# Turning four of eight token tiles to channel layout with VectorE block transposes and SBUF transfers in the w_out stage

## The chip, the cores and the metric

The kernel runs on one core of one Trainium2 chip. The core has five engines that run side by side and meet through semaphores: TensorE (matmuls and transposes, with a separate weight load), VectorE, ScalarE, GpSimd and SyncE. Here SyncE (queue SP) issues nearly all DMAs. Each engine takes its instructions in the order in which they were put on its queue. The metric is the device time of one execution in microseconds (us), as the median over runs.

## The reference, cut to what matters

One layer of a hybrid decoder over 1024 tokens with 16 meta tokens ahead of them, 1024 channels, float32. Two mixers (convolution and windowed attention) are merged by gates; then

```python
mixed = jax.nn.sigmoid(g_attn) * y_attn + jax.nn.sigmoid(g_conv) * y_conv
h = layer_norm(DEEPNORM_ALPHA * h + mixed @ w_out, ln1_g, ln1_b)
up = causal_dwconv(h @ ffn_w_up, ffn_dw, ffn_dw_b)
u, g = jnp.split(up, 2, axis=-1)
f = (jax.nn.gelu(g, approximate=False) * u) @ ffn_w_down
return layer_norm(DEEPNORM_ALPHA * h + f, ln2_g, ln2_b)
```

The norm runs over the channels of a token, so it wants tokens on the partitions. The product with `ffn_w_up` sums over channels, so it wants channels on the partitions. Between the two, `h` is turned.

## The kernel before, in words

A float32 product is done as three products of parts rounded to a shorter form (high by high, high by low, low by high; `product`, lines 304 to 316). Splitting a tensor into its parts is a cast on ScalarE and a subtraction on VectorE.

The stage around the change is the product with `w_out`. The 1024 tokens make eight tiles of 128, taken in the order 3, 7, 2, then two edge rows (called -1), then 6, 0, 4, 1, 5 (line 1480). For one tile, `out_rows` (line 1319) does this:

- it loads the residual rows from `h0d` into one of two row buffers `RT`, which is `OB` columns 0 to 2047, the two taken in turn, so that the load for a tile needs the buffer of the tile two before it;
- TensorE makes two halves of 512 columns, 24 matmuls each, into a PSUM bank `ps_w` (three banks in turn);
- VectorE adds each half to the residual (L1342) and takes its statistics (L1343); the norm follows: aggregate (L246), reciprocal root on ScalarE (L253), three small steps (L261 to L263) and the scaling (L1364);
- SyncE stores the rows to `h1d`.

`turn` (line 1373) then turns the tile: eight 128x128 transposes on TensorE (L1378) into two PSUM banks `ps_h`, and eight activations on ScalarE (L1388) that read them, apply the norm's gain and bias per channel and write `FA`, the channel layout `h1F`. The loop hands a finished tile to the next call of `out_rows` (`ahead`), so a tile is turned while TensorE works on the next one: after that one's first half, tile 3 after the second half. Tile 5, the last, is turned inside the next stage.

The next stage multiplies by `ffn_w_up` with a seven-product scheme on 2x2 blocks. It needs sums and differences of the blocks of `FA` (`form_t2`, `form_t3`, `form_t4`, L1288) and their parts (`bsplit`: cast L1279, subtraction L1284). The tokens stand in two halves, sub 1 (tiles 2, 3, 6, 7) and sub 0 (tiles 0, 1, 4, 5; its first columns, `EARLY`, are tiles 0 and 4). These steps run during the products of tiles 0, 4, 1 and 5 (the `work` table, line 1476), with the first weight splits (L1409, L1426). The first products of the next stage (L1599) are those of sub 1; those of sub 0 follow.

Order: every instruction carries a priority number (`rank`; `RK_TURN` is 450, lower goes first), from which a planner with its own time model puts each engine's instructions in order. `line` (line 1257) fixes the order of a list of VectorE instructions by hand: those of tiles 0, 4, 1, 5, the splits and the sums stand in it. `after` fixes the order of two instructions on one engine. `load` (line 112) issues a DMA on SyncE's queue.

Of the kernel before, what the change touches and what calls it, by code (L numbers as in the profile page):

```python
# [25 lines left out]
AF = mybir.ActivationFunctionType  # L26
# [3 lines left out]
P = 128  # L30
D = 1024
KC = D // P
# [29 lines left out]
SUB = [(0, 258), (258, HW)]  # L62


RK_TURN, RK_SPLIT, RK_EVAC, RK_START, RK_QKV, RK_RESID, RK_ATT = 450, 500, 600, 1000, 10000, 20000, 30000
# [36 lines left out]
def tile_hybrid_layer(  # L102
# [3 lines left out]
    nc = tc.nc  # L106
# [5 lines left out]
    def load(o, i):  # L112
        return nc.sync.dma_start(out=o, in_=i)
# [5 lines left out]
    def f32(ap):  # L119
        return ap.bitcast(F)  # L120

    def after(ins, first):

        tc.add_manual_dep(ins.ins, first.ins.name, mybir.DependencyInfo(
            mybir.DependencyClass.NoSync, mybir.DependencyReason.SCHED_ONLY), reason="order of work")

    @contextmanager
    def rank(p):

        saved = tc.cur_priority  # L130
        tc.cur_priority = p
        yield
        tc.cur_priority = saved
# [10 lines left out]
    RHC = arena.tile([P, 8384], R, name="RHC")  # L144
    RHO = arena.tile([P, 8384], R, name="RHO")
    OB = arena.tile([P, 4 * U], F, name="OB")
# [49 lines left out]
    cols = const.tile([P, N_COLS], F, name="cols")  # L196
# [19 lines left out]
    g1col = lambda k: colA[:, 58 + k:59 + k]  # L216
    b1col = lambda k: colA[:, 66 + k:67 + k]
# [60 lines left out]
    def split(raw, hi, lo, quick=False, behind=None):  # L278
        ins = nc.scalar.copy(hi, raw)  # L279
        if behind is not None:  # L280
            after(ins, behind)
        return (nc.vector if quick else nc.gpsimd).tensor_tensor(lo, raw, f32(hi), OP.subtract)  # L282
# [391 lines left out]
    bias = ap.tile([P, 2, NH // 2, KW], F, name="bias")  # L674
# [58 lines left out]
    for r in range(2):  # L733
        rows = slice(r * HD, (r + 1) * HD)
# [13 lines left out]
    src = ps[:16, :P].rearrange("p (g d) -> p g d", d=HD)  # L748
    nc.scalar.copy(VA[:16, 0, :, 0], src)
    nc.vector.tensor_tensor(VA[:16, 0, :, 1], src, f32(VA[:16, 0, :, 0]), OP.subtract)  # L750
    for q4 in range(2):
# [4 lines left out]
        src = ps[:, :].rearrange("p (n g d) -> p n g d", g=2, d=HD)  # L756
# [16 lines left out]
    def load_q(g, i):  # L773
        m = 0 if i else 16
        t = ap.tile([P, 8 * P + 16], R, name="qt", tag="qt", bufs=3)[:, 16 - m:]
        for h in range(2):
            load(f32(t[h * HD:(h + 1) * HD]), dram(qd, g * HD * 8 * U + q_at(i) - m, [[8 * U, HD], [1, 8 * P + m]]))
        if m:
            pairs0.append(t[:, :16].rearrange("p (l r q) -> p l r q", l=2, r=4))
        return t[:, m:].rearrange("p (u l h x) -> p l u h x", l=2, u=2, h=2)  # L780
# [7 lines left out]
    ahead = chunks_done[first_chunk + 2 * KC + 7]  # L788
# [6 lines left out]
    for h in range(NH):  # L795
        g, r = divmod(h, 4)
        o = ps[:2, h * 16:(h + 1) * 16]
# [34 lines left out]
    for g in range(NKV):  # L832
# [3 lines left out]
        src = ps[:16].rearrange("p (r q) -> p r q", r=4)[:, :, 0:2]  # L836
# [3 lines left out]
    for g in range(NKV):  # L840
        o = po[:, g * 8:g * 8 + 8]
# [21 lines left out]
    for i in range(NB):  # L863
        for g in range(NKV):
            q = load_q(g, i) if i else q0[g]
# [6 lines left out]
            for u in range(2):  # L872
# [3 lines left out]
                for h in range(2):  # L876
                    o = ps[:, h * KW:h * KW + w]
# [8 lines left out]
                if not i:  # L886
                    f = first[u]
                    src = ps[:, :2 * KW].rearrange("p (h c) -> p h c", h=2)
# [9 lines left out]
            for h in range(2):  # L898
                for u in range(2):
                    j = h * 2 + u  # L900
# [68 lines left out]
    OC = late.tile([P, 8320], R, name="OC")  # L969
# [169 lines left out]
    def two_rows(k, behind=None):  # L1139

        for t, a in enumerate(two_sum):
            m = pair[:, k, t:t + 1]
            if k == 0:
                nc.scalar.activation(a, wo_raw[k], AF.Copy, scale=m)
                continue
            ins = nc.vector.scalar_tensor_tensor(a, wo_raw[k], m, a, OP.mult, OP.add)
            if behind is not None:
                after(ins, behind)
# [74 lines left out]
    def h1_at(sub, i):  # L1223
        return 2048 * sub + i * (SUB[sub][1] - SUB[sub][0])

    def h1F(sub, h, k):
        o = h1_at(sub, h * KC + k)
        return FA[:, o:h1_at(sub, h * KC + k + 1)]
# [28 lines left out]
    def line(ins):  # L1257

        if lined:
            after(ins, lined[-1])  # L1260
        lined.append(ins)
        return ins
# [33 lines left out]
    def form_t2(sub, cs=slice(None)):  # L1296
        b11, b12, b21, b22 = blocks(sub)
        bsub(b11, b12, b11, cs)
        bsub(T2_AT[:, :b22.shape[1]], b22, b11, cs)

    def form_t3(sub, cs=slice(None)):
        b11, b12, b21, b22 = blocks(sub)
        bsub(b12, b22, b12, cs)

    def form_t4(sub, cs=slice(None)):
        b11, b12, b21, b22 = blocks(sub)
        bsub(b21, T2_AT[:, :b22.shape[1]], b21, cs)

    def split_of(sub, q, cs=slice(None)):
        b11, b12, b21, b22 = blocks(sub)  # L1310
        src = {B11: b11, B21: b21, BT2: T2_AT[:, :b22.shape[1]], BT4: b21, BT1: b11, BT3: b12, B22: b22}[q]
        bsplit(sub, q, src, cs)
# [76 lines left out]
        return behind[-1] if behind else None  # L1389


    RING = [RHO[:, i * 1024:(i + 1) * 1024] for i in range(4)]
    RING += [None] * 4
    RING += [RHO[:, 6208 + i * 1024:6208 + (i + 1) * 1024] for i in range(2)]
    ring_next, W2 = [0], []

    def wsplit(src):
# [4 lines left out]
        else:  # L1402
            i = (i - 2) % len(RING)
            if RING[i] is None:
                RING[i] = wsp_p.tile([P, D], R, name="ws", tag=("whi", "wlo")[i % 2])
            t = RING[i]
        hi, lo = t[:, 0:512], t[:, 512:1024]
# [59 lines left out]
    def edges():  # L1467
        with rank(RK_TURN):
            first, second = (FA[:, h * 2064:h * 2064 + 2064].rearrange("p (k n) -> p k n", n=258)[:, :, 0:2]
                             for h in range(2))  # L1470
            for t, c, op in ((edge, 58, OP.mult), (first, 66, OP.add)):
                line(nc.vector.tensor_tensor(first, t, colA[:, c:c + KC].unsqueeze(2).to_broadcast([P, KC, 2]), op))
            nc.vector.memset(second, 0.0)

    ahead = []
# [4 lines left out]
    for i in (3, 7, 2, -1, 6, 0, 4, 1, 5):  # L1480
        if i == -1:
            out_rows(i)
            continue
        rows = out_rows(i, ahead, work.get(i, ()))
        ahead = [None, (i, *rows)] if i == 3 else [(i, *rows)]
        if i == 3:
            two_rows(7, rows[2])
        if i == 7:
            for a, (hi, lo) in zip(two_sum, two_parts):
                after(split(a, hi, lo, True), rows[2])  # L1490
            two_stack.close()
            W2.append(wo_stack.enter_context(tc.tile_pool(name="w2", bufs=1, side="right", reuse_waits="tile")).tile(
                [P, 2048], R, name="W2"))
        if i == 0:
            form_t2(1)
        if i == 4:
            split_of(1, BT4)
            split_of(1, BT1)
            edges()
        if i == 1:  # L1500
            split_of(1, BT3)
            split_of(0, B21, EARLY)
            form_t3(0, EARLY)
            form_t4(0, EARLY)
# [64 lines left out]
    for c in range(FC):  # L1569
# [8 lines left out]
        for subs in passes:  # L1578
            last = subs == passes[-1]
            w_next = iter(range(7))  # L1580
            a, b = SUB[subs[0]][0], SUB[subs[-1]][1]
            i = max(a, 2)

            def at(t, a=a):
                return t[:, 254 + a:254 + b]
# [19 lines left out]
            def tt(*x):  # L1605
                with rank(RK_CHAIN):
                    return nc.vector.tensor_tensor(*x)
# [12 lines left out]
            ins = tt(c11[:, a:b], at(Z), u13[:, a:b], OP.add)  # L1620
# [23 lines left out]
            ins = tt(c22[:, i:b], c22[:, i:b], u13[:, i:b], OP.add)  # L1644
# [127 lines left out]
    rows, stats = {}, {}  # L1772
# [158 lines left out]
```

## Time and profile before

| | |
|---|---|
| time, median of 3 runs | 1236.12 us (1236.04 to 1236.16) |
| the profiled execution: span from its first to its last instruction | 1234.6 us |
| what a run's time has beside that span | 1.5 us (1236.12 - 1234.6) |
| TensorE busy | 1225.2 us, 99% |
| VectorE busy | 1085.2 us, 88% |
| ScalarE busy | 584.7 us, 47% |
| GpSimd busy | 15.6 us, 1% |
| mean granted TensorE clock | 0.999 |

The profile gives no time of its own for the profiled execution other than the span. In its lines PE is TensorE, PEld its weight load, DVE is VectorE, ACT ScalarE, POOL GpSimd, SPq the queue of SyncE; L1378 is line 1378 of the kernel. A row of a timeline has the start, the duration, the engine, the line, the operation, output from input, shapes and a count, and in brackets the idle time before it and what ended it. A busy share is an average over the whole span; the chain that ended last says what a change in one place can be worth.

### The profile page before, as it was taken

How to read it: one execution, taken by the hardware profiler on the slowest of the kernel's cores; microseconds unless marked ns; L12 is line 12 of the kernel's file. 1: busy time of each engine (PE TensorE's matmuls, PEld its weight loads, DVE VectorE, ACT ScalarE, POOL GpSimd, SP SyncE). 2: the span in 40 equal slices, each digit the busy share in tenths (PEclk: the TensorE clock that was granted, in tenths of full speed). 3: DMA queues.
4: the chain of work that ended last, by engine and by line, in shares of the span. 5: the costliest groups of instructions: out<-in, count | busy, mean ns of one | idle time of the engine just before them, and what ended most of it. 6: DMA issues, size and time to landing. Idle time of an engine off the chain costs nothing.

```text
span 1234.6 us, 21810 instructions
## 1 busy us (share of the span) xinstructions
PE 1225.2 (99%) x8568; PEld 1141.5 (92%) x8568; DVE 1085.2 (88%) x1842; ACT 584.7 (47%) x1065; POOL 15.6 (1%) x20
## 2 busy tenths in 40 slices
PE   9999999999999999999999999999999999999997
PEld 8999989999999999888999999999999998888886
DVE  8899989999879798659899999998999986996697
ACT  7532336654255223345755545555455554445331
POOL 1000000000000010000000000000000000000000
PEclk9999999999999999999999999999999999999999
DMA  7396834412255655322255555554455568988722
GB/s 282 74 298 151 210 98 116 127 55 73 82 158 163 183 140 144 104 85 87 66 171 207 191 187 205 188 183 142 172 203 190 178 239 304 391 315 312 256 86 85
DMA packets 109152, 213.02 MB, mean 173 GB/s; under 512 B 31883, under 2 KB 46779, under 8 KB 108922
## 3 DMA queue, kind: packets, MB, share of 16 engines
q1 hardware_dynamic: 93050, 200.56, 49.5%
q10 hardware_dynamic: 16000, 11.07, 2.9%
q8 instruction: 67, 1.10, 0.4%
q14 instruction: 35, 0.29, 0.1%
HBM read 149.98 MB, written 62.70 MB: 172 GB/s over the span
## 4 chain that ended last, share of the span: by engine, by line
PE 98%; DVE 1%; ACT 0%; issue 0%; DMA 0%; POOL 0%; DVEq 0%; POOLq 0%
PE px L1599 14%; PE py L1599 9%; PE ps_x L1745 9%; PE ps_z L315 8%; PE ps_z L314 8%; PE ps_z L310 8%; PE ps_z L1745 8%; PE pw L1599 5%; PE pz L1599 5%; PE ps_p L310 2%; PE ps_p L314 2%; PE ps_p L315 2%; PE ps_w L310 2%; PE ps_w L315 2%; PE ps_w L314 2%; PE ps_z L550 2%
## 5 line engine op out<-in xcount | busy, mean ns | idle before, releaser
L707 DVE SCALAR_TENSOR_TENSOR FA<-cin,cols,FA 128x1026 f32<-128x1026 f32 x120 | 152.2, 1277 | 0.9
L315 PE MATMUL ps_z<-RHO,wlo 128*128 128x256 f32 (+2 forms) x324 | 103.5, 320 | 0.0
L314 PE MATMUL ps_z<-RHO,whi 128*128 128x256 f32 (+2 forms) x324 | 103.4, 319 | 0.0
L315 PE MATMUL ps_z<-RHC,wlo 128*128 128x256 f32 (+2 forms) x324 | 103.4, 319 | 0.0
L314 PE MATMUL ps_z<-RHC,whi 128*128 128x256 f32 (+2 forms) x324 | 103.4, 319 | 0.0
L310 PE MATMUL ps_z<-RHO,whi 128*128 128x256 f32 (+2 forms) x324 | 103.3, 319 | 0.0
L310 PE MATMUL ps_z<-RHC,whi 128*128 128x256 f32 (+2 forms) x324 | 103.2, 319 | 0.0
L279 ACT CAST whi<-wr 128x1024 fp32r<-128x1024 f32 x37 | 38.9, 1050 | 107.4 <-PE ps_z L314 85.5
L1408 ACT CAST RHO<-wr 128x512 fp32r<-128x512 f32 x92 | 55.3, 619 | 25.3 <-DVE wr L1426 11.7
L1409 DVE TENSOR_TENSOR RHO<-wr,RHO 128x512 fp32r<-128x512 f32 x92 | 61.8, 684 | 5.1 <-ACT RHO L1408 5.0
L310 PEld LDWEIGHTS ps_z<-RHO,whi 128*128 128x128 f32 x324 | 60.9, 188 | 4.3
L314 PEld LDWEIGHTS ps_z<-RHO,whi 128*128 128x128 f32 x324 | 61.0, 188 | 4.2
L310 PEld LDWEIGHTS ps_z<-RHC,whi 128*128 128x128 f32 x324 | 60.9, 188 | 4.1
L314 PEld LDWEIGHTS ps_z<-RHC,whi 128*128 128x128 f32 x324 | 61.0, 188 | 4.0
L315 PEld LDWEIGHTS ps_z<-RHO,wlo 128*128 128x128 f32 x324 | 60.9, 188 | 4.0
L315 PEld LDWEIGHTS ps_z<-RHC,wlo 128*128 128x128 f32 x324 | 61.0, 188 | 3.9
L1426 DVE TENSOR_TENSOR wr<-wr 128x512 f32<-128x512 f32 x88 | 59.9, 681 | 0.2
L282 DVE TENSOR_TENSOR wlo<-wr,whi 128x1024 fp32r<-128x1024 f32 x35 | 42.7, 1220 | 11.8 <-ACT whi L279 11.4
L1611 ACT COPY FA<-px 128x514 f32<-128x514 f32 (+2 forms) x23 | 13.2, 572 | 70.7 <-PE px L1599 70.6
L1408 ACT CAST ws<-wr 128x512 fp32r<-128x512 f32 x60 | 36.1, 618 | 18.8 <-DVE wr L1426 10.7
L714 ACT ACTIVATE FA<-ps_z,cols 128x258 f32<-128x258 f32 (+2 forms) x48 | 26.1, 544 | 39.4 <-PE ps_z L315 36.6
L1599 PE MATMUL px<-OA,RHO 128*128 128x258 f32 (+1 forms) x336 | 43.8, 279 | 0.0
(491 smaller groups left out, 3488.2 us busy)
## 6 DMA issues: line engine op xcount, KB each, us to landing
wr<-in_w_up_dram SPq DMA_DIRECT2D x44, 512.0 KB, 4.6
wr<-in_w_z_dram SPq DMA_DIRECT2D x30, 512.0 KB, 3.9
fd<-FA SPq DMA_DIRECT2D x44, 256.0 KB, 2.4
OB<-in_w_down_dram SPq DMA_DIRECT2D x19, 512.0 KB
qt<-qd SPq DMA_DIRECT2D x28, 256.0 KB, 4.1
td<-OB SPq DMA_DIRECT2D x12, 512.0 KB
sums<-fd SPq DMA_DIRECT2D x12, 512.0 KB, 7.6
sd<-sums SPq DMA_DIRECT2D x12, 512.0 KB
```

The costliest lines, as they stand in the source:

```text
L279: ins = nc.scalar.copy(hi, raw)
L282: return (nc.vector if quick else nc.gpsimd).tensor_tensor(lo, raw, f32(hi), OP.subtract)
L310: ins = nc.tensor.matmul(ps, ah, bh, start=i == 0, stop=False)
L314: nc.tensor.matmul(ps, ah, bl, start=False, stop=False)
L315: last = nc.tensor.matmul(ps, al, bh, start=False, stop=i == n - 1)
L707: nc.vector.scalar_tensor_tensor(acc[c], cin[:, j:j + U], wc, acc[c], OP.mult, OP.add)
L714: nc.scalar.activation(t, ps, AF.Tanh, bias=bcol(14 + i), scale=0.5)
L1408: nc.scalar.copy(hi, src)
L1409: ins = nc.vector.tensor_tensor(lo, src, f32(hi), OP.subtract)
L1426: ins = nc.vector.tensor_tensor(*x)
L1599: ins = nc.tensor.matmul(o, x[:, ks], bmat(sub, q, hl, k), start=first and k + j == 0, stop=k == 3 and j == 2, skip_group_check=not first)
L1745: nc.tensor.matmul(bank[:, cs], l[:, ts], r[:, ws], start=first and a and x + k == 0, stop=z and x == len(ops) - 1 and k == 2, skip_group_ ...
```

## The change

Tiles 3, 7, 2 and 0 (`TURN_AT`) are no longer turned by `turn`. For them `turn_dma` issues, right after `out_rows`:

1. one VectorE transpose of the 128x1024 row tile in 32x32 blocks, from the row buffer into 1024 columns of `OB` (from column 2048 for tiles 3, 7 and 2, from column 3072 for tile 0), its blocks grouped by the group q of 32 channels; for tile 0 it stands in the fixed order `line`;
2. 16 DMAs on SyncE's queue, each of 32 partitions by 256 columns (1 KB a row), that move the block rows of 32 tokens to the partitions of their 32 channels, into free columns of `OC` or `RHC`;
3. eight ScalarE activations as before, which now read those columns in SBUF, in four runs of 32, in place of PSUM.

Tiles 6, 4, 1 and 5 are turned as before. Tile 3 no longer asks for the later place of its turn.

```diff
+    TURN_AT = {3: (OC, 4144, 2048), 7: (OC, 5168, 2048), 2: (OC, 6192, 2048), 0: (RHC, 2096, 3072)}
+
+    def turn_dma(i, r):
+        t, o, b = TURN_AT[i]
+        blocks, cols = OB[:, b:b + 1024], f32(t[:, o:o + 1024])
+        with rank(RK_TURN):
+            ins = nc.vector.transpose(blocks.rearrange("p (q k j) -> p q k j", q=4, k=KC),
+                                      r.rearrange("p (k q j) -> p q k j", k=KC, q=4))
+            if i in (0, 4):
+                line(ins)
+            for a in range(4):
+                for q in range(4):
+                    load(cols[32 * q:32 * q + 32, a * 256:(a + 1) * 256],
+                         blocks[32 * a:32 * a + 32, q * 256:(q + 1) * 256])
+            h, jj = divmod(i, 4)
+            sub = 0 if jj < 2 else 1
+            a = 2 + jj * P - SUB[sub][0]
+            src = cols.rearrange("p (a k j) -> p k a j", a=4, k=KC)
+            for k in range(KC):
+                nc.scalar.activation(h1F(sub, h, k)[:, a:a + P].rearrange("p (a j) -> p a j", a=4), src[:, k],
+                                     AF.Identity, bias=b1col(k), scale=g1col(k))
+
...
         rows = out_rows(i, ahead, work.get(i, ()))
-        ahead = [None, (i, *rows)] if i == 3 else [(i, *rows)]
+        ahead = [] if i in TURN_AT else [(i, *rows)]
+        if i in TURN_AT:
+            turn_dma(i, rows[0])
         if i == 3:
             two_rows(7, rows[2])
```

## The prediction

> **What bounds the kernel now.** I read the page first (engine shares, then the chain that ended last), then the pieces of that chain between 517 and 606 us, then the same stretch engine by engine.
>
> ```profile
> span 1234.6 us, 21810 instructions
> ...
> PE 1225.2 (99%) x8568; PEld 1141.5 (92%) x8568; DVE 1085.2 (88%) x1842; ACT 584.7 (47%) x1065; POOL 15.6 (1%) x20
> ...
> PE 98%; DVE 1%; ACT 0%; issue 0%; DMA 0%; POOL 0%; DVEq 0%; POOLq 0%
> ...
> 517.40 0.87 PE ps_h L1378 x8
> 522.38 0.87 PE ps_h L1378 x8
> 547.84 0.88 PE ps_h L1378 x8
> 559.62 0.87 PE ps_h L1378 x8
> ...
> 605.53 1.57 PE pw L1599 x11
> ```
>
> TensorE is 98% of the chain, and every group of eight transposes (one token tile, L1378) lies on it with 0.87 to 0.88 us. So a transpose that leaves TensorE shortens the chain, until another engine takes its place. In this stretch VectorE stands close behind:
>
> ```profile
> 512.69 2.47 DVE L1146 SCALAR_TENSOR_TENSOR two<-wr,pair,two 128x1024 f32<-128x1024 f32 x2
> ...
> 519.20 0.81 DVE L1364 TENSOR_SCALAR OB<-OB,mv,sd 128x1024 f32<-128x1024 f32 x1
> 534.10 0.81 DVE L1364 TENSOR_SCALAR OB<-OB,mv,sd 128x1024 f32<-128x1024 f32 x1
> 542.42 0.69 DVE L1342 TENSOR_TENSOR OB<-ps_w,OB 128x512 f32<-128x512 f32 x1 [4.91 <-PE ps_w L315]
> 547.88 0.69 DVE L1342 TENSOR_TENSOR OB<-ps_w,OB 128x512 f32<-128x512 f32 x1 [2.03 <-PE ps_w L315]
> 549.21 1.27 DVE L1409 TENSOR_TENSOR W<-wr,W 128x512 fp32r<-128x512 f32 x2
> 550.41 2.35 DVE L1284 TENSOR_TENSOR OC<-FA,OC 128x1024 fp32r<-128x1024 f32 x2
> 554.22 0.69 DVE L1342 TENSOR_TENSOR OB<-ps_w,OB 128x512 f32<-128x512 f32 x1 [0.32 <-PE ps_w L315]
> 586.73 0.68 DVE L1409 TENSOR_TENSOR RHO<-wr,RHO 128x512 fp32r<-128x512 f32 x1
> 589.56 0.69 DVE L1342 TENSOR_TENSOR OB<-ps_w,OB 128x512 f32<-128x512 f32 x1 [2.15 <-PE ps_w L315]
> 605.53 1.57 PE L1599 MATMUL pw<-OA,RHO 128*128 128x258 f32 x11 [0.38 <-DVE OA L1284]
> ```
>
> In the second fence (the timelines of VectorE and TensorE: start, us, what) the bracket is the idle time before an instruction. Up to 548 VectorE has gaps of 2 to 5 us in which it waits for TensorE. From 548 on it has only 0.32 at 554 and 2.15 at 589.56, beside short waits for ScalarE inside each norm. At 605.53 it is TensorE that waits, 0.38 us, for a split by VectorE. So both engines arrive at 605 together: the gain is the smaller of what TensorE and VectorE save ahead of it.
>
> **The change part by part.** *TensorE.* Four groups go (tiles 3, 7, 2, 0): 0.87 + 0.87 + 0.88 + 0.87 = 3.49 us. (Tile 2's group, near 536, is not among the rows shown; I give it the 0.88 of its neighbour.) Nothing takes their place on TensorE. Tiles 6, 4, 1, 5 keep theirs. This is the whole possible gain: no other TensorE work is touched.
>
> *ScalarE.* The same eight activations a tile, reading SBUF in four runs of 32 in place of PSUM:
>
> ```profile
> 531.10 0.29 ACT L253 ACTIVATE sd<-mv,eps 128x1 f32<-128x1 f32 x1
> 536.53 2.90 ACT L1388 ACTIVATE FA<-ps_h,cols 128x128 f32<-128x128 f32 x8 [2.17 <-PE ps_h L1378]
> 539.29 2.03 ACT L1279 CAST OC<-FA 128x1024 fp32r<-128x1024 f32 x2
> 558.81 1.05 ACT L1279 CAST OC<-FA 128x1024 fp32r<-128x1024 f32 x1 [2.60 <-DVE FA L1288]
> 575.12 0.67 ACT L1279 CAST RHC<-FA 128x520 fp32r<-128x520 f32 x1
> ```
>
> 2.90 us a tile, bounded by 2 us below and 4 above; ScalarE is 47% busy, with gaps of 2 to 3 us, so I cost it at nothing except for its place in the latency below.
>
> *VectorE.* Four new 32x32 block transposes of 128x1024. None is in the trace. Rows of that size are 0.81 (one source, L1364) and 1.22 to 1.24 (two sources, L1284 and L1146, here shown as pairs of 2.35 and 2.47); twice the slower would be 2.4. I take 1.2, since nothing says that the block transpose gets the quicker pace of L1364. Those of tiles 3, 7, 2 fall in the stretch with gaps of 4.9 us and cost nothing. Tile 0's is put in VectorE's written order ahead of form_t2(1), at about 557, in the full stretch. The account there: TensorE comes 3 x 0.87 = 2.6 us earlier to 547.88 and 3.5 earlier to 589.56. VectorE was done at 587.41 (586.73 + 0.68); with start 2.6 earlier and 1.2 more it is done at 586.0, and TensorE's last product is there at 589.56 - 3.5 = 586.1. It fits with 0.1 to spare: at 2.4 us it would lose 1.1.
>
> The Trainium skill ("VectorE: DVE Perf Modes", section "The three transpose paths") gives 311 ns for VectorE's 128x128 and 390 ns for TensorE's, both bf16. By that a tile would be an estimated 8 x 0.311 = 2.5 us on VectorE and the sum 1.2 us worse; the same page's 390 ns is not what these chains show (0.87 / 8 = 0.11 us each), so I read its figures as single instructions with their fixed cost.
>
> *SyncE.* Each turned tile issues 16 DMAs of 32 rows x 1 KB on SP's queue, 64 in all, at high rank behind the tile's h1d store and ahead of the h0d load two tiles on (which needs the same row buffer).
>
> ```profile
> 512.80 0.32 SPq L113 DMA_DIRECT2D h1d<-OB  x1
> 518.31 0.32 SPq L113 DMA_DIRECT2D OB<-h0d  x1
> 536.23 0.24 SPq L113 DMA_DIRECT2D ed<-OB  x1
> 539.60 0.33 SPq L113 DMA_DIRECT2D OB<-h0d  x1
> L113 SPq DMA_DIRECT2D tab<-in_table_dram x1: 356/356/356, 10.5 to 10.5; - x1
> L113 SPq DMA_DIRECT2D va<-va x2: 680/798/917, 95.9 to 96.6; - x2
> 146.28 2.37 SPq L113 DMA_DIRECT2D qt<-qd  x4
> qd<-qsl SPq DMA_DIRECT2D x15, 128.0 KB, 2.4
> OB<-h0d SPq DMA_DIRECT2D x8, 512.0 KB, 3.2
> ```
>
> A plain 128-row DMA occupies the queue for 0.32, two rows 0.24, 33 rows (tab) 0.36, 64 rows 0.62 from start to start (2.37 for four), and a strided SBUF to SBUF one 0.8. For 32 rows with the gap behind it I take p = 0.43 (tab's 0.36 and 0.07), between 0.32 and 0.8. A tile is then L = 16p = 6.9 us, against 10.9 us of products per tile (559.62 - 547.84 from one group of transposes to the next, less 0.88): the queue keeps up. Landing I take at 2.4 (qsl), a row load at 3.2.
>
> What counts is the chain of latencies, since tiles 3, 7 and 2 share one block buffer (OB from 2048): a transpose must wait until the DMAs before it have landed. Tile 3 is normed at 512.7, transposed at 513.9; its DMAs go out from 514.0, land by 514 + L + 2.4 = 523.3. Tile 7's transpose waits for that (VectorE idles there anyway; behind it stands L1342 of tile 2, which comes late by some 3 us, and TensorE has three PSUM banks to run on). Tile 7's DMAs land at 520.1 + 2L = 533.9; tile 2 is normed by 533.2 (534.10 + 0.81, less two groups of transposes), so its DMAs start at 521.4 + 2L = 535.2. Behind them (and one 0.3 store) goes tile 0's h0d load, which lands at 524.9 + 3L = 545.6. VectorE wants it at 547.88 - 2.6 = 545.3, with the 0.3 us gap of 554.22 to spare: just in time. Each 0.1 us more in p is 48 x 0.1 = 4.8 us later, all of it on VectorE's full stretch.
>
> Tile 2's data land at 521.4 + 2L + L + 2.4 = 544.5, say 544.8 with the store between; eight activations to 547.7, the first cast (1.05) to 548.8. VectorE wants that split at 550.41 - 2.6 = 547.8. So it is 1.0 late; the gap at 554 takes 0.3 and the spare above 0.1: I charge 0.6.
>
> Tile 0's own DMAs (from 556 to 563, landed 565.4, activated by 568.3) are needed by the EARLY split (the cast of 575.12) only near 575.1 - 3.5 = 571.6: covered, with 3 us in hand.
>
> *Transfers.* 2 MB more within SBUF. The stretch with most of it, by stretches of 15 us (busy us and count of PE, PEld, DVE, ACT, POOL; clock, DMA share, GB/s):
>
> ```profile
> 515.00:530.00 15.00, 15.00 (x76) 11.84 (x75) 7.90 (x14) 8.39 (x22) 0.00 (x0) 1.00 0.41 140
> 530.00:545.00 15.00, 15.00 (x72) 12.37 (x71) 8.52 (x22) 6.47 (x15) 0.00 (x0) 1.00 0.29 72
> ```
>
> The DMA engines are busy 0.41 and 0.29 of the time, so the traffic itself costs nothing. POOL's queue is not touched.
>
> **Sum.** -3.5 (TensorE) + 0 (VectorE) + 0.6 (late split) = -2.9 on the profiled span of 1234.6: 1231.7. The median of the runs, 1236.12, lies 1.5 us above that span, so the time is 1233.2. A measurement of this kernel can tell about 0.2% from no change, 2.5 us: faster begins below 1233.6.
>
> **Rivals.**
>
> *A, forecast:* transfers hidden but for the late split, 1233.2; own range 1232.6 (nothing late) to 1233.6 (1 us late).
>
> *B, an engine queue held up by the transfers' landing:* ScalarE takes its instructions in order, and the activations of a DMA-turned tile stand in the same queue as the norm's reciprocal root (L253). If the schedule puts tile 7's activations (data at 533.9) ahead of tile 2's root (531.1 before, wanted near 529.4), that root waits until 533.9 + 2.9 = 536.8, tile 2's norm ends some 3 us later than 533.9, and the whole chain behind with it: 3 us lost of 2.9, time about 1236.1 at worst and 1235 if part is absorbed: I put it at 1235.7. For it: high rank for both, and the row at 536.53, where ScalarE now waits 2.17 us with nothing ahead. Against it: ScalarE's gaps, and the order may well be drawn up with these landings in mind.
>
> *C, slower: SP's issue is the bound.* At the 64-row price, p = 0.62, L = 9.9 and tile 0's load lands at 554.6, 9.3 us after it is wanted; 0.3 absorbed; VectorE's full stretch carries 9 us to 605 against 3.5 saved: +5.5, 1241.6. It turns from gain to loss where 48p - 20.7 exceeds 3.5, at p = 0.504. For it: the 64-row and SBUF to SBUF rows are all above that. Against it: rows with 33 and fewer partitions are below 0.4, and they are the nearest in form.
>
> The Trainium skill speaks for C: "DMA: Bandwidth & Descriptors", section "Bandwidth", calls transfers under 64 KB descriptor-dominated and asks for 1 MiB; these are 32 KB. The trace's 2-row and 128-row issues (0.24, 0.32) say the price per DMA hardly depends on size, which agrees with the rule's drift but not with a ruin.
>
> *D, the transpose takes 2.4 us, twice L1284:* VectorE ends its stretch 1.2 us later than in A: 1234.4. For it: four-byte data through a path that no row shows. Against it: no VectorE row of 128x1024 is above 1.24.
>
> **How the numbers follow.** A 0.47, B 0.20, C 0.27, D 0.06. The predicted time is A's. Faster by over 0.2% (below 1233.6) is A alone, 0.47. C begins at p = 0.45, where A's own range ends; up to p = 0.556 (2.5 us slower) it still lies within 0.2%, and I give that part 0.06. So within 0.2% are B, D and that part, 0.32; slower is the rest of C, 0.21. A, B, D and mild C lie within 1232.6 to 1238.6; I leave 0.6 below for what ScalarE may save in reading SBUF, and stop at 1238.8, which leaves out about 0.2.
>
> **What the changed profile would show.** Right: half of the 64 transposes of L1378 left, and no such group at 517, 522, 536 and 560; four VectorE transposes of 1.2 us; 16 SP rows of a tile in about 7 us; VectorE's last L1342 (589.56) about 3 us earlier; TensorE's wait ahead of pw still below 1 us. B: L253 released by a DMA-fed L1388. C: VectorE's L1342 of tile 0 waiting for DMA OB<-h0d, by microseconds, and TensorE waiting more than 0.38 ahead of pw. D: the transpose row itself. Most likely to be wrong is p, and the order that the schedule gives ScalarE and SP.

## The result and the profile after

The changed kernel takes 1252.43 us against 1236.09: 1.013 times as long (95% interval 1.0118 to 1.0142), 16.3 us lost where 2.9 were to be gained. The forecast of 1233.2 and its range up to 1238.8 were both wrong. The place was among the rivals (C, SyncE's queue), at a larger price than any given there. The profiled span grew by 15.8 us (1250.4 - 1234.6).

The page of the changed kernel (span, busy time, the chain that ended last):

```profile
span 1250.4 us, 21869 instructions
...
PE 1226.0 (98%) x8536; PEld 1140.5 (91%) x8536; DVE 1089.2 (87%) x1846; ACT 586.6 (47%) x1065; POOL 15.6 (1%) x20
...
PE 91%; SPq 3%; DVE 3%; DMA 1%; issue 1%; ACT 0%; POOL 0%; DVEq 0%; POOLq 0%
```

SPq, which was not in the chain before, now has 3% of it, and TensorE has fallen from 98% to 91%. VectorE's share grew too, from 1% to 3%, but its busy time hardly did (1085.2 to 1089.2). Between 516 and 555 us the chain follows the issues of tiles 3, 7 and 2 on SyncE's queue, with a landing and a block transpose between one tile and the next, and from 571 to 581 the issues of tile 0. SyncE's queue in a timeline (start, us, what; idle time is left out there):

```profile
512.58 0.32 SPq L113 DMA_DIRECT2D h1d<-OB  x1
...
516.20 10.30 SPq L113 DMA_DIRECT2D OC<-OB  x16
526.60 0.53 SPq L113 DMA_DIRECT2D h1d<-OB  x1
527.16 0.43 SPq L113 DMA_DIRECT2D OB<-h0d  x1
529.38 10.01 SPq L113 DMA_DIRECT2D OC<-OB  x16
...
543.51 10.01 SPq L113 DMA_DIRECT2D OC<-OB  x16
553.57 1.21 SPq L113 DMA_DIRECT2D edge<-ed  x2
554.87 0.52 SPq L113 DMA_DIRECT2D h1d<-OB  x1
555.44 3.17 SPq L113 DMA_DIRECT2D OB<-h0d  x2
```

The same transfers as a group, by their tile (fastest/mean/slowest ns of one issue, first and last, idle time):

```profile
L113 SPq DMA_DIRECT2D OC<-OB x48: 507/588/599, 516.2 to 552.9; - x48
```

The 16 issues of a tile take 10.0 to 10.3 us, 0.63 us from start to start (0.588 and a gap). Right behind them other issues take longer as well: the h1d store, 0.32 us by itself at 512.58, takes 0.52 to 0.53. The h0d load of tile 0, issued at 539.60 before, goes out at 555.44. VectorE, ScalarE and TensorE behind it (timelines; the bracket is the idle time before):

```profile
514.86 1.24 DVE L1398 STREAM_TRANSPOSE OB<-OB 128x1024 f32<-128x1024 f32 x1
528.10 1.25 DVE L1398 STREAM_TRANSPOSE OB<-OB 128x1024 f32<-128x1024 f32 x1 [6.43 <-DMA OC<-OB]
560.63 0.69 DVE L1342 TENSOR_TENSOR OB<-ps_w,OB 128x512 f32<-128x512 f32 x1 [10.94 <-DMA OB<-h0d]
563.16 2.36 DVE L1284 TENSOR_TENSOR OC<-FA,OC 128x1024 fp32r<-128x1024 f32 x2
582.57 0.49 ACT L1411 ACTIVATE FA<-RHC,cols 128x128 f32<-128x128 f32 x1 [0.81 <-DMA RHC<-OB]
583.28 0.16 DVE L261 SCALAR_TENSOR_TENSOR sd<-mv,sd 128x1 f32<-128x1 f32 x1 [1.02 <-ACT sd L253]
583.86 0.81 DVE L1364 TENSOR_SCALAR OB<-OB,mv,sd 128x1024 f32<-128x1024 f32 x1
584.82 1.94 PE L1378 MATMUL ps_h<-cols,OB 128*128 128x128 f32 x8 [11.78 <-DVE OB L1364]
605.36 0.69 DVE L1342 TENSOR_TENSOR OB<-ps_w,OB 128x512 f32<-128x512 f32 x1 [2.86 <-PE ps_w L315]
```

Tile 0's first add stood at 547.88 and is now at 560.63, after 10.94 us of waiting for its rows. From there VectorE's full stretch runs nearly as before, 13 us late, with two additions ahead of tile 4's norm: tile 0's own block transpose, and a wait of 1.02 us for the reciprocal root (0.36 before). That root stands on ScalarE's queue behind the first activation of tile 0 (582.57), which waited for tile 0's DMAs. TensorE does not see the lateness until 573; then the next thing on its queue is the turn of tile 4, whose norm VectorE ends at 584.67, and TensorE stands still for 11.78 us. The turn itself takes 1.94 us where it took 1.04, as this row of the kernel before shows:

```profile
571.24 1.04 PE L1378 MATMUL ps_h<-cols,OB 128*128 128x128 f32 x8
```

A table of the windows says why (window; its length; busy us and count of PE, PEld, DVE, ACT, POOL; granted clock, that is the share of full speed that TensorE was given; DMA share; GB/s):

```profile
570.00:575.00 5.00, 3.04 (x14) 2.19 (x12) 4.91 (x6) 2.09 (x2) 0.00 (x0) 1.00 0.37 131
575.00:580.00 5.00, 0.00 (x0) 0.00 (x0) 4.83 (x7) 1.85 (x3) 0.00 (x0) 0.58 0.21 52
580.00:585.00 5.00, 0.18 (x1) 0.21 (x2) 3.80 (x9) 3.48 (x8) 0.00 (x0) 0.50 0.43 131
585.00:590.00 5.00, 5.00 (x18) 4.28 (x18) 4.66 (x8) 4.09 (x12) 0.00 (x0) 0.56 0.59 206
590.00:605.00 15.00, 15.00 (x72) 12.50 (x71) 11.05 (x19) 6.67 (x15) 0.00 (x0) 1.00 0.21 72
```

After the wait TensorE computes at half pace: its matmuls stand 0.43 us apart until 589.5, and 0.23 from there on. Two distances show how the loss adds up. The turn of tile 4 begins 13.58 us later than before (584.82 against 571.24), and tile 5's last add comes 15.80 us later (605.36 against 589.56). So 13.6 us are VectorE's lateness, and 2.2 us are lost behind that turn, at the slow clock; run 6 below wins 2.5 us there. Two smaller stalls of TensorE lie near 530 (13.72 and 13.10 us busy of 15 in the windows from 515 and 530). The chain does not pass through them: from 511 to 584 it has no piece of TensorE, so time lost near 530 only shortens the wait at 573.

### The profile page after: what moved, and what is told of

The parts are those of the page before. It is cut to its first block, busy times and chain, and to the rows that moved or that the text cites. A ratio compares the mean times of both kernels' runs of the same rounds, so it can differ in the third digit from the quotient of the medians.

```text
span 1250.4 us, 21869 instructions
## 1 busy us (share of the span) xinstructions
PE 1226.0 (98%) x8536; PEld 1140.5 (91%) x8536; DVE 1089.2 (87%) x1846; ACT 586.6 (47%) x1065; POOL 15.6 (1%) x20
## 4 chain that ended last, share of the span: by engine, by line
PE 91%; SPq 3%; DVE 3%; DMA 1%; issue 1%; ACT 0%; POOL 0%; DVEq 0%; POOLq 0%
PE px L1623 14%; PE py L1623 9%; PE ps_x L1769 9%; PE ps_z L315 8%; PE ps_z L314 8%; PE ps_z L310 8%; PE ps_z L1769 7%; PE pw L1623 5%; PE pz L1623 5%; SPq L113 3%; PE ps_p L310 2%; PE ps_p L314 2%; PE ps_p L315 2%; PE ps_z L550 2%; PE ps_o L928 1%; PE ps_s L879 1%
## 5 line engine op out<-in xcount | busy, mean ns | idle before, releaser
L1431 DVE TENSOR_TENSOR ws<-wr,ws 128x512 fp32r<-128x512 f32 x60 | 40.7, 689 | 4.0 <-ACT ws L1430 3.9
```

The lines of the kernel that those rows point to most:

```text
L1431: ins = nc.vector.tensor_tensor(lo, src, f32(hi), OP.subtract)
```

## The experiments

Theory S: the 16 issues of a tile fill SyncE's in-order queue for 10 us, and the residual rows and the turned data come late behind them. The rivals: V, the new work on VectorE and ScalarE, or another order of work; W, the waits for the one block buffer; B, bytes and not issues. K is an addition to S: part of the loss is the clock after the wait. In each set the kernel before ran beside the others on the same chip.

**1. Without the transfers.** The activations read the block-transposed rows where VectorE left them.

```diff
-            for a in range(4):
-                for q in range(4):
-                    load(cols[32 * q:32 * q + 32, a * 256:(a + 1) * 256],
-                         blocks[32 * a:32 * a + 32, q * 256:(q + 1) * 256])
+            cols = blocks
```

> The changed kernel without its 64 transfers: ScalarE reads the block-transposed rows where VectorE left them (so the blocks of channels and tokens are mixed up; all other work is kept). Theory S (the 16 issues of a tile, 0.63 us each, hold up SyncE's queue for 10 us and with it the residual rows and the turned data): all the loss goes and TensorE's 3.5 us come out, 1232.6 us (1232.0 to 1234). Theory V (VectorE's and ScalarE's own new work, or another order of work, is what costs): still above 1240. Theory W (waits for the one shared block buffer): it goes too, since a read by ScalarE frees the buffer in 3 us, so this run does not tell S from W.

Measured: 1234.28 against 1236.18, ratio 0.9983 (0.9974 to 0.9993). All of the loss is the transfers', as S and W say; V falls for the 16 us. But 1.9 us come out and not 3.5. TensorE's timeline tells where the other 1.6 went: a wait of 1.31 at tile 4's turn, where there was none before, and at the top of the next stage a wait of 0.79, where 0.38 was lost before (at 605.53).

The rows of run 1:

```profile
554.73 1.25 DVE L1398 STREAM_TRANSPOSE OB<-OB 128x1024 f32<-128x1024 f32 x1
568.86 1.07 PE L1378 MATMUL ps_h<-cols,OB 128*128 128x128 f32 x8 [1.31 <-DVE OB L1364]
597.38 1.64 PE L1620 MATMUL py<-RHC,ws 128*128 128x256 f32 x12 [0.79 <-ACT OB L1632]
```

Tile 0's block transpose, 1.25 us in VectorE's full stretch, makes tile 4's norm late for its turn by 1.31. So V has a share in the missing 1.6 us, though none in the 16.

**2. The transfers as a load only.** TensorE turns all eight tiles; the block transposes and transfers stay, unread.

```diff
-        ahead = [] if i in TURN_AT else [(i, *rows)]
+        ahead = [None, (i, *rows)] if i == 3 else [(i, *rows)]
...
-            for k in range(KC):
-                nc.scalar.activation(h1F(sub, h, k)...
```

> The changed kernel with TensorE's turn of all eight tiles put back; the four block transposes and the 64 transfers stay, but nothing reads what they bring. S: the residual rows still stand behind the issues on SyncE's queue, VectorE still waits for tile 0's rows some 10 us, and the 3.5 us of TensorE are paid again: 1250 to 1256. V with the late data as the cause (the activations and splits that wait for turned data, and not the rows): the rows are a side matter, 1237 to 1241.

Measured: 1249.6, ratio 1.0106 (1.0091 to 1.0121). Nobody waits for the turned data here, and tile 0's add still waits 10.14 us for its rows:

```profile
560.61 0.69 DVE L1342 TENSOR_TENSOR OB<-ps_w,OB 128x512 f32<-128x512 f32 x1 [10.14 <-DMA OB<-h0d]
```

So the late rows alone suffice to carry most of the loss (13.4 us of 16.3). It is a little below S's 1250, although TensorE's 3.5 us are paid again.

**3. A second block buffer.**

```diff
-    TURN_AT = {3: (OC, 4144, 2048), 7: (OC, 5168, 2048), ...
+    TURN_AT = {3: (OC, 4144, 2048), 7: (OC, 5168, 3072), ...
...
-            whole = OB[:, 3072:4096]
+            whole = FA[:, 1024:2048]
```

> The changed kernel with a second block buffer: tile 7's blocks go to the columns that tile 0 uses later, the edge rows' scratch moves out of the way. S: SyncE's queue stays full, only the idle gaps in it between the tiles' groups (2 to 3 us each, two of them) close: 1247 to 1250. W: the transposes of tiles 7 and 2 no longer wait 6.4 and 3.3 us for the landing, so the chain is 8 to 10 us shorter: 1240 to 1245.

Measured: 1258.35, ratio 1.018 (1.0164 to 1.0195): slower than the changed kernel, against both expectations. SyncE's queue says why:

```profile
516.29 20.43 SPq L113 DMA_DIRECT2D OC<-OB  x32
536.76 0.59 SPq L113 DMA_DIRECT2D h1d<-OB  x1
537.39 2.85 SPq L113 DMA_DIRECT2D OB<-h0d  x2
```

With its buffer free, tile 7's 16 issues follow tile 3's at once, and the rows of tiles 2 and 6 stand behind 32 issues in place of 16. The wait that W blames had let the rows of tile 2 through. So W's forecast is refuted: with that wait gone the kernel is 5.9 us slower. The trace shows S's mechanism, rows behind issues, in a way that I had not foreseen, though S's number was missed too. The waits for the buffer are still a part of how the lateness adds up: in the changed kernel the issues of tiles 7 and 2 begin only when those of the tile before have landed.

**4. Fewer issues, through DRAM.** The blocks go out to a tensor in DRAM (`bd`) in one store and come back in four loads.

```diff
-            for a in range(4):
-                for q in range(4):
-                    load(cols[...], blocks[...])
+            load(bd[i], blocks)
+            for q in range(4):
+                load(cols[32 * q:32 * q + 32].rearrange("p (a c) -> p a c", a=4),
+                     bd[i].rearrange("(a p) (q c) -> q p a c", a=4, q=4)[q])
```

> The changed kernel with five transfers a tile in place of 16: the blocks are stored to DRAM in one and loaded back in four, 32 partitions of four runs of 1 KB each. S: issue falls from 10 us a tile to about 3 (0.32 + 4 x 0.65), though the loads wait on the queue for the store to land (about 2.5 us): tile 0's rows come near the time at which VectorE wants them, 1233 to 1238. W: the store frees the block buffer within 3 us, so it gives the same. V: no gain, above 1245.

Measured: 1249.11, ratio 1.0105 (1.0088 to 1.0122). S and W both said 1233 to 1238 and missed. V's "above 1245" fits the number, but run 1 has ruled V out for the 16 us. SyncE's queue is free most of the time, and the time is hardly better. The queues of SyncE, ScalarE and VectorE (lines are one further down than in the changed kernel):

```profile
540.58 1.74 SPq L113 DMA_DIRECT2D OC<-bd  x4
545.79 3.18 ACT L1412 ACTIVATE FA<-OC,cols 128x128 f32<-128x128 f32 x8 [9.47 <-DMA OC<-bd]
549.19 0.16 DVE L262 SCALAR_TENSOR_TENSOR sd<-mv,sd 128x1 f32<-128x1 f32 x1 [7.88 <-ACT sd L254]
```

The activations of tile 2 stand on ScalarE's queue ahead of tile 6's reciprocal root; they wait 9.47 us for their data, and VectorE waits 7.88 for the root. That is the mechanism of the forecast's rival B, at a larger price. So S is not all there is to a slow turn: what a late turn holds up depends on which queue its reader stands in.

**5. The same number of issues, a quarter of the bytes.** The rest of the turned columns keeps old data.

```diff
-                    load(cols[32 * q:32 * q + 32, a * 256:(a + 1) * 256],
-                         blocks[32 * a:32 * a + 32, q * 256:(q + 1) * 256])
+                    load(cols[32 * q:32 * q + 32, a * 256:a * 256 + 64],
+                         blocks[32 * a:32 * a + 32, q * 256:q * 256 + 64])
```

> The changed kernel with as many transfers, each a quarter of the bytes (32 rows of 256 B; the rest of the turned columns keeps old data). Theory S (the number of issues on SyncE's queue, whatever they carry): 1250 to 1253, no change from the changed kernel's 1252.4, and 0.58 to 0.63 us from issue to issue. Theory B (bytes, the DMA engines or SBUF's side of them): most of the 16 us comes back, below 1242.

Measured: 1251.14, ratio 1.0122 (1.0108 to 1.0136).

```profile
516.49 10.29 SPq L113 DMA_DIRECT2D OC<-OB  x16
```

10.29 us for 16 issues, whether they carry 512 KB or 128. B is refuted. The Trainium skill's rule that small transfers are descriptor-dominated ("DMA: Bandwidth & Descriptors", section "Bandwidth") agrees so far: a quarter of the bytes in as many rows took as long. What this run measures is the price of an issue on the queue; how it changes with the number of rows was not tested.

**6. A filler in TensorE's wait.** 48 needless matmuls ahead of tile 4's turn.

```diff
+            if i == 4:
+                fill = pat.tile([P, 512], F, name="ps_f", tag="o", bufs=1)
+                for _ in range(48):
+                    behind.append(nc.tensor.matmul(fill, mixed(5, 0, 0), wo[0][0][:, 0:512], start=True, stop=True))
+                    after(behind[-1], behind[-2])
```

> The changed kernel with 48 needless matmuls of 128x512 (48 x 0.227 = 10.9 us) on TensorE's queue just ahead of the turn of tile 4, where TensorE stood idle for 11.8 us and then ran 10 us at a granted clock near 0.55. Theory K (part of the loss is the clock after the idle time): the filler hides in the wait, the clock stays at 1.0, and the time falls by 2 to 3 us, to 1249.5 to 1250.5. Theory S alone (VectorE's late stretch sets the end, and TensorE's clock is a side matter): 1252 to 1253.

Measured: 1249.89, ratio 1.0111 (1.0097 to 1.0125).

```profile
572.83 11.04 PE L1378 MATMUL ps_f<-OA,RHO 128*128 128x512 f32 x48
584.76 1.07 PE L1383 MATMUL ps_h<-cols,OB 128*128 128x128 f32 x8 [0.89 <-DVE OB L1364]
```

And its table by windows, right behind the wait:

```profile
585.00:590.00 5.00, 5.00 (x28) 4.25 (x27) 4.97 (x9) 4.58 (x13) 0.00 (x0) 1.00 0.60 212
```

The turn of tile 4 begins at the same time (584.76 and 584.82), takes 1.07 us in place of 1.94, and the clock is 1.00. From that turn to tile 5's last add it is 18.36 us, as in the kernel before (18.32) and not 20.54 as in the changed one. The time falls by 2.5 us (1252.43 less 1249.89; the kernel before took 1236.09 and 1236.16 beside them): K holds, at a price of 2.2 to 2.5 us.

**7. Half the issues on ScalarE's queue.**

```diff
-                    load(cols[32 * q:32 * q + 32, a * 256:(a + 1) * 256],
+                    (load, store)[q % 2](cols[32 * q:32 * q + 32, a * 256:(a + 1) * 256],
```

> The changed kernel with eight of a tile's 16 transfers issued on ScalarE's queue instead of SyncE's. Theory S: SyncE's share falls to 5 us a tile and tile 0's rows come some 15 us earlier, near the time they are wanted; ScalarE is held 8 x 0.6 = 5 us a tile ahead of its roots and activations: 1236 to 1244. If the sum of issues counts whatever the queue: 1250 to 1254.

Measured: 1244.52, ratio 1.0064 (1.0049 to 1.0079), 0.5 above S's range and far from 1250. With half of the issues on the other queue half of the loss goes (8.2 us are left of 16.3). An issue costs as much on ScalarE's queue (0.60 us, the median of the 24 of tiles 3, 7 and 2) as on SyncE's (0.59), so by these medians the two queues hardly slow each other. Tile 0's add comes at 549.34, 11 us earlier and not 15, and TensorE's wait at tile 4's turn falls from 11.78 to 9.21.

**8. The rows out of the way.**

```diff
-            load(whole, h0d[u:u + n, :])
+            store(whole, h0d[u:u + n, :])
```

> The changed kernel with the residual rows' loads issued on ScalarE's queue, so that they no longer stand behind the 16 transfers of a tile. If the late rows are what delays VectorE: the 10.9 us idle ahead of tile 0's add go, but tile 2's turned data still land near 555 and the split of them is wanted at 548: 1246 to 1249. If the turned data alone are the limit: 1250 to 1253. If the rows alone were: below 1241.

Measured: 1249.29, ratio 1.01 (1.0083 to 1.0117), 0.3 above the first expectation.

```profile
548.19 0.69 DVE L1342 TENSOR_TENSOR OB<-ps_w,OB 128x512 f32<-128x512 f32 x1 [4.09 <-DMA OB<-h0d]
560.95 2.36 DVE L1284 TENSOR_TENSOR OC<-FA,OC 128x1024 fp32r<-128x1024 f32 x2 [10.14 <-ACT OC L1279]
```

Tile 0's add comes at 548.19 in place of 560.63, but the first split now waits 10.14 us for its cast, which waits for tile 2's turned data. It ran at 563.16 in the changed kernel and runs at 560.95 here. Runs 2 and 8 together show that rows and turned data are late by nearly the same, and that curing one leaves the other. The next of VectorE's additions stands behind that split, and TensorE waits 2.96 us for it. Its granted clock stays at 1.00 in the window behind that wait:

```profile
565.10 0.50 PE L310 MATMUL ps_w<-RX,RHO 128*128 128x512 f32 x1 [2.96 <-DVE OB L1342]
```

```profile
566.00:568.00 2.00, 2.00 (x11) 1.64 (x10) 1.50 (x6) 0.29 (x1) 0.00 (x0) 1.00 0.00 0
```

**9 and 10. One tile alone.**

```diff
-    TURN_AT = {3: (OC, 4144, 2048), 7: (OC, 5168, 2048), 2: (OC, 6192, 2048), 0: (RHC, 2096, 3072)}
+    TURN_AT = {0: (RHC, 2096, 3072)}
```

(and the same with `{3: (OC, 4144, 2048)}`; `ahead` keeps the later place of tile 3's turn)

> Only tile 0 leaves TensorE, by block transpose and 16 transfers; 3, 7 and 2 are turned by TensorE again. Chain theory (each tile's 10 us of issue delays the next tile's transpose and rows, and the delay adds up over 3, 7, 2): one tile alone has slack for most of it: -0.9 for TensorE, +1.3 for VectorE's transpose in its full stretch, up to 1 us for late rows of tile 1: 1236 to 1238. Linear theory (each tile costs a quarter of 16 us): 1240.

> Only tile 3 leaves TensorE, as in the changed kernel. Chain theory: tile 2's rows come 8 to 9 us late, as in the changed kernel (531), TensorE runs out of PSUM banks for about 2 us near 530, and VectorE has caught up by tile 0: -0.9 + 2 = 1237 (1236 to 1238.5). Linear theory: 1240.

Measured: tile 0 alone 1240.16, ratio 1.0029 (1.0019 to 1.0038); tile 3 alone 1241.86, ratio 1.0039 (1.0026 to 1.0052). Both are above what the chain theory said and near the linear one. Tile 3's timelines, and a window of it:

```profile
528.05 3.18 ACT L1411 ACTIVATE FA<-OC,cols 128x128 f32<-128x128 f32 x8 [2.30 <-DMA OC<-OB]
531.14 0.56 ACT L1355 COPY OB<-ps_w 2x512 f32<-2x512 f32 x1
531.47 1.29 DVE L1342 TENSOR_TENSOR OB<-ps_w,OB 128x512 f32<-128x512 f32 x2 [9.78 <-DMA OB<-h0d]
531.75 1.08 PE L1353 MATMUL ps_w<-OC,sel 128*2 128x512 f32 x4 [3.21 <-ACT OB L1355]
```

```profile
534.00:536.00 2.00, 2.00 (x6) 1.51 (x6) 2.00 (x5) 0.29 (x1) 0.00 (x0) 0.50 0.00 0
```

Tile 0's, in the same two views:

```profile
571.24 0.49 ACT L1411 ACTIVATE FA<-RHC,cols 128x128 f32<-128x128 f32 x1 [1.58 <-DMA RHC<-OB]
571.95 0.16 DVE L261 SCALAR_TENSOR_TENSOR sd<-mv,sd 128x1 f32<-128x1 f32 x1 [1.80 <-ACT sd L253]
573.49 1.06 PE L1378 MATMUL ps_h<-cols,OB 128*128 128x128 f32 x8 [2.75 <-DVE OB L1364]
```

```profile
574.00:576.00 2.00, 2.00 (x10) 1.68 (x8) 2.00 (x6) 1.97 (x6) 0.00 (x0) 0.61 0.65 262
```

With tile 3 alone, tile 2's first add comes 9 us later (531.47 against 522.42 before), as I had said, and TensorE runs out of PSUM banks for 3.21 us. Two of the three banks wait for these rows. The third waits for ScalarE's copy of the edge rows (531.14), which stands on ScalarE's queue behind tile 3's eight activations, and those waited for tile 3's DMAs. What I had also left out is the clock: 0.50 after that wait. VectorE does catch up (its wait ahead of tile 0's add is 2.03 us again).

With tile 0 alone, no late rows hold VectorE up. Tile 4's norm is late for its turn by 2.75 us: 1.31 is what run 1 showed for the block transpose, and the other 1.44 come from the root, for which VectorE waits 1.80 in place of 0.36 because it stands behind tile 0's first activation. The clock falls to 0.61 behind that. So a turned tile costs through ScalarE's queue as well as through SyncE's, which neither theory had, and these two runs do not tell the chain theory from the linear one.

**11 and 12. Two or three tiles through DRAM, with ScalarE's order set by hand.** The activations of a turned tile are put behind the norm's root of the next one.

```diff
-    TURN_AT = {3: (OC, 4144, 2048), 7: (OC, 5168, 2048), 2: (OC, 6192, 2048), 0: (RHC, 2096, 3072)}
+    TURN_AT = {3: (OC, 4144, 2048), 7: (OC, 5168, 2048)}
...
+                after(nc.scalar.activation(...), roots[-1])
```

(with the transfers of experiment 4; then the same with tile 2)

> Only tiles 3 and 7 leave TensorE, through DRAM in five transfers a tile, and their activations on ScalarE stand behind the norm's reciprocal root of the next tile; tiles 2 and 0 are turned by TensorE again. If S and the order of ScalarE's queue are the whole trouble: nothing is late, 2 x 0.87 us come out, 1234.4 (1234.0 to 1234.9). If something else in the change costs, above 1235.5.

> The same with tile 2 too. 3 x 0.87 us come out if tile 2's data come by 545, 1233.5; they pass a store and a load, some 9 us from the end of tile 2's norm at 533, and the activations and the cast need 4 us more, against 547.8 when VectorE wants them: up to 1.5 us late, so 1233.5 to 1235.5. If ScalarE's queue were still held up as in the run with all four tiles through DRAM (7.9 us idle on VectorE), above 1238.

Measured: 1237.33, ratio 1.0013 (1.0004 to 1.0022), with two tiles; 1241.13, ratio 1.0039 (1.0026 to 1.0051), with three. Neither gains; both fall on the second branch of their expectation. In the kernel with two tiles the planner also reordered TensorE's first products (tile 3's adds, at 507.01 before, come at 509.63), and the root of tile 6 is held up behind the activations of tile 7:

```profile
509.63 1.89 DVE L1345 TENSOR_TENSOR OB<-ps_w,OB 128x512 f32<-128x512 f32 x3 [4.44 <-PE ps_w L318]
543.94 3.19 ACT L1415 ACTIVATE FA<-OC,cols 128x128 f32<-128x128 f32 x8 [3.09 <-DMA OC<-bd]
547.35 0.16 DVE L264 SCALAR_TENSOR_TENSOR sd<-mv,sd 128x1 f32<-128x1 f32 x1 [3.62 <-ACT sd L256]
```

With three tiles VectorE waits 2.48 us for that root, 6.07 for tile 2's rows and 3.60 for the cast of the first split. VectorE's order changed too: with two tiles tile 7's norm, which began at 517.53 before, stands behind a wait of 5.43 us for tile 2's rows and begins after 527. So these two runs do not test SyncE's issues and ScalarE's order alone, and what the reordering costs was not tested by itself.

No version tried that turns all tiles beats the kernel before. Run 1, without the transfers, shows what four tiles in this order of work could bring if their transfers cost nothing: 1.9 us.

## Why the prediction was wrong, point by point

- *TensorE's saving, 3.49 us:* right in size. The four groups are gone, and in run 1, where nothing is late, tile 0's first add came 2.9 us earlier (544.95 against 547.88) after three of them; 0.2 of that was there at 510.4 already, ahead of the first.
- *VectorE's transpose at 1.2 us:* right in size (1.24, 1.25), though it was a choice between two paces and not a measured row. Rival D had it at 2.4. The Trainium skill's 311 ns for a 128x128 ("VectorE: DVE Perf Modes", section "The three transpose paths"), taken eight times, would be an estimated 2.5; the trace does not agree, and 128x1024 in one instruction takes half of that.
- *VectorE at nothing, "fits with 0.1 to spare":* wrong by 1.3. I had measured VectorE's spare time at tile 5's last add, where it waits for TensorE. But TensorE meets VectorE earlier, at tile 4's turn, and there was almost no spare time there: before the change the norm ended at 570.69 (569.88 + 0.81) and the turn began at 571.24, right behind TensorE's last product.
- *The issue price p = 0.43:* this is the step that failed. It was read from tab's row (33 rows, 0.36 us, DRAM to SBUF), and the queue was said to keep up with 6.9 us a tile. It measured 0.588 and a gap, 0.63 from start to start, so a tile took 10 us, and tile 0's rows went out at 555.44. The rows that I had put against it, 64 rows (0.62) and SBUF to SBUF (0.8), were on the right side of the 0.504 at which gain turns to loss. Why tab's price does not hold is open. Tab is a single issue, and these stand 16 in a row, behind which even the h1d store takes 0.52 in place of 0.32. The kernel before had a row of issues too, which I did not use: nine from DRAM at 0.65 each (`89.46 5.86 SPq L113 DMA_DIRECT2D bias<-vd  x9`). Four loads from DRAM in a row of 32 partitions each took 0.44 a start in run 4 (1.74 for four). So neither the count of rows nor the source gives the price by itself.
- *The chain of latencies:* its form was right, its size too small even with the right p. With p = 0.63 it gives 555.1 for tile 0's rows; they were there at 560.6. What it lacked: tile 3's transpose was put behind two other instructions (514.86 in place of 512.7), the edge loads and tile 6's store went ahead of the rows (553.57 to 555.4), and two row loads went out together (the first landed 5.1 us after its issue, by the chain, in place of 3.2). One term erred the other way: the transfers within SBUF landed 1.8 us after their issue, not 2.4.
- *Rival C's price, 1241.6:* too low by 11 us. Six of them are that lateness of the rows (560.6 against 554.6). About 2.2 are the clock behind TensorE's wait at tile 4's turn, and 0.8 are what VectorE loses between tile 0's add (12.75 us late) and that turn (13.58 us late), to tile 0's transpose and the root. The remaining 1.8 are not taken apart; C had taken 3.8 off for saved transposes and a gap.
- *Tile 0's own DMAs, "covered, with 3 us in hand":* wrong in the place. I had looked at the split that needs tile 0's data. But ScalarE's queue put the first activation of tile 0 ahead of tile 4's root, and the root had to wait for the DMAs: 0.66 us in the changed kernel (1.02 against 0.36), 1.44 in run 9.
- *Rival B:* its mechanism is that same wait, so it did happen in the changed kernel, at a small price and for another tile than the one named. In run 4 it cost VectorE a wait of 7.88 us.

## What to carry to other kernels

Price a transfer by the queue that issues it as well as by its bytes: 16 issues at 0.63 us held SyncE's queue for 10 us a tile, and everything behind them (rows for the next tile but one, stores) moved by as much. Take the price of an issue from rows in which as many stand one behind the other, and let the range reach to the ends of all rows when the forecast turns on that price. Ask what stands behind the reader of a late transfer on the reader's own queue. When TensorE's work is moved to an engine that runs nearly full beside it, look for the first place where TensorE waits for that engine, not for the last; and count what TensorE loses after a wait, not only in it.

## What the runs showed of the hardware that I had not expected

- A DMA of 32 rows of 1 KB within SBUF takes 0.59 us on the queue when 16 stand in a row, on SyncE's queue as on ScalarE's (run 7), and a quarter of the bytes takes as long (run 5). 128 rows of 4 KB to DRAM take 0.32 alone and 0.52 to 0.53 right behind such a row.
- TensorE's granted clock was 0.61 in the window after a wait of 2.75 us (run 9), 0.50 after one of 3.21 (run 10) and 0.50 after one of 11.78, each time for 4 to 5 us of work, and then 1.00 again. But a wait of 2.96 us in run 8 left it at 1.00. So the length of the wait alone did not decide it near 3 us, and what else did is open. The Trainium skill ("TensorE: Matmul & The Clock Gate", section "Why this matters for your kernels") warns of gaps above some 3 us; the waits of 3.21 and 11.78 agree, and the one of 2.75 is shorter and slowed the clock all the same.
